# A hybrid decoder layer on one core: dilated attention as near blocks and far token classes, joined by an exchange of maxima and sums

## The chip, the cores and the metric

The kernel runs on one core of a Trainium2 chip. The metric is the device time of one execution in microseconds (us). TensorE multiplies matrices into PSUM, VectorE and ScalarE empty PSUM and do the elementwise work, GpSimd (POOL) works on SBUF, and SyncE (SP) issues the DMAs from one queue.

## The reference

One layer on 1024 tokens with 1024 channels in float32: a pre-norm, one projection into a gated part (256 channels) and the q, k and v of 12 attention heads of 64, an output projection, and a gated convolutional channel mixer. The change touches the attention only:

```python
DILATED_CONFIGS = ((128, 1), (512, 4), (2048, 16))
...
for window, dil in DILATED_CONFIGS:
    o, lse = dilated_segment(q, k, v, rel_bias, window, dil)   # causal; query t attends t, t-d, ..., t-window
    ...
w = jax.nn.softmax(jnp.stack(lses, axis=0), axis=0)
return jnp.sum(w[..., None] * o, axis=0)
```

Combining the three segments by their softmax denominators is one softmax over all keys, in which a key at distance d counts as often as segments contain it: (d <= 128) + (d divisible by 4 and d <= 512) + (d divisible by 16). The count's logarithm is added to the logit with the relative-position bias. So a query sees every token of the last 128 and, farther back, only tokens whose distance is divisible by 4. With 1024 tokens, d divisible by 16 is never cut off.

## The kernel before, in words

Numbers are split into a high and a low part of TensorE's fp32r type, so that products are made of two or three matmuls. After the norm and the transposes of x (hT), the kernel makes the gated part and v (`proj_a`, eight token blocks of 24 matmuls for each half of the v heads, `v_out`), in which three matmul pairs (`bias_mm`) make a table of bias by distance; it is stored in DRAM (`gd`), and `bias_copies` spreads each head's row over 128 rows (`gcop`), from which `load_bias` reads a skewed 128 x 1024 tile.

Then attention runs head by head. `proj_qk` is a list of 48 matmuls of 512 columns (two halves of the tokens, hf 0 and 1, 24 each) which make q and k of one head; after the 24th and the 48th, `evac` empties them and two DMAs copy Kh and Kl to the other 64 partitions. These matmuls are the fill: `pump(n)` puts the next n of them into TensorE's order, at places given by the tables FILL and FILL_AT, so that TensorE has work while other engines finish something. `qk_row` makes the scores of a block of 128 queries with all earlier keys (128 to 1024 columns, in pieces of up to 512), VectorE adds the bias and takes the maximum (L523), ScalarE exponentiates and sums (L528), VectorE takes the reciprocal (L530), POOL rescales the row (L531). `tpv` transposes the weights in batches of up to four blocks (`trans`, L551), splits them (pth, ptl, L555 and L556) and multiplies with v (`pv`, L573) for 256 queries at a time. Scores run one group of two blocks ahead of the values. In heads 10 and 11 `load_wo` brings the output weights through two staging buffers (`raw`), and the first tile of the output projection (`wout_mm`, L630) is the fill of head 11.

The order on TensorE and on SP is the program's own order (`manual_schedule(engines={ET.PE, ET.SP})`); for the other engines a planner orders the instructions ahead of time, and each engine then runs its list strictly in turn.

Of the kernel before, what the change touches and what calls it, by code (L numbers as in the profile page):

```python
# [24 lines left out]
F = mybir.dt.float32  # L26
# [17 lines left out]

FILL = ((0, 11), (4, 6, 3), (3, 7, 2, 4), (0, 3, 2, 1, 2))
FILL_AT = {0: ((9, 4), (4, 2, 5), (6, 2, 5, 0), (0, 1, 4, 1, 5)),
# [3 lines left out]
FILL_FIRST = 4  # L50

# [4 lines left out]
WO_AT = {0: (0, 1), 1: (), 2: (2, 3), 3: (4, 5), 4: (6, 7)}  # L56

L = 1152
NCOP = 128
# [3 lines left out]
def build(tc, x, g1, g2, g3, g4, w_in, ln_g, ln_b, sp_w, sp_b, rel, w_out, w_gate, w_up,  # L63
# [28 lines left out]
    with tc.manual_schedule(engines={ET.PE, ET.SP}), \  # L92
# [39 lines left out]
        ones = cp.tile([1, 128], F, name="ones")  # L132
# [7 lines left out]
        gcop = dr.tile([HEADS, NCOP, L], F, name="gcop")  # L140
# [224 lines left out]
        def bias_load():  # L365
            for c in range(3):
                b = mtile("bb%d" % c)
                sp.dma_start(b[0:32, 0:384], onehot[:, c * 384:(c + 1) * 384])
                sp.dma_start(b[0:12, 384:768], lnm[:, c * 384:(c + 1) * 384])
                sp.dma_start(b[0:32, 768:780], rel)  # L370
                BB.append(b)

        def bias_mm(c):
            b = BB[c]
            p = bS("bias%d" % c)
            pe.matmul(p[:12, :384], b[0:32, 768:780], b[0:32, 0:384], start=True, stop=True)
            dve.tensor_add(b[0:12, 384:768], p[:12, :384], b[0:12, 384:768])

        def bias_store():
            for c in range(3):  # L380
                sp.dma_start(gd[:, c * 384:(c + 1) * 384], BB[c][0:12, 384:768])

        def bias_copies(h):
            sp.dma_start(gcop[h], bass.AP(tensor=gd.tensor, offset=gd.offset + h * L, ap=[[0, NCOP], [1, L]]))

        def v_out(vg, i, p):
            for j in range(3):
# [6 lines left out]
                dve.tensor_sub(vt[:, 1:3, :], src, vt.bitcast(F)[:, 0:4:3, :])  # L394

# [28 lines left out]
        for i in range(NT):  # L424
# [13 lines left out]
            if i in (0, 2, 5):  # L438
                bias_mm(i // 2)
# [7 lines left out]
        def load_qk(h):  # L447
# [7 lines left out]
            for s in range(2):  # L455
                wh = ap.tile([128, 512], R, tag="wqh", name="wqh%d_%d" % (h, s), bufs=4)
                wl = ap.tile([128, 512], R, tag="wql", name="wql%d_%d" % (h, s), bufs=4)
                split(wh, wl, r[:, s * 512:(s + 1) * 512], ENG[WQK_HI[s]], pool)
                WQ[h].append((wh, wl))

        def load_bias(h):
            b = ap.tile([128, T], F, tag="bias", name="bias%d" % h, bufs=2)
            for a in range(0, 128, NCOP):
                sp.dma_start(b[a:a + NCOP], bass.AP(tensor=gcop.tensor, offset=gcop.offset + h * NCOP * L + 127 - a,
                                                    ap=[[L - 1, NCOP], [1, T]]))
            BIAS[h] = b

        def proj_qk(h):
# [15 lines left out]
            def evac(hf):  # L484
                if hf == 0:
                    QK[h] = tuple(ap2.tile([128, T], R, tag="qk", name="%s%d" % (n, h), bufs=4)
                                  for n in ("Q", "Kh", "Kl"))
                q, kh, kl = QK[h]
                p = st[hf]
                s = slice(hf * 512, (hf + 1) * 512)  # L490
                act.activation(kh[64:128, s], p[64:128], AF.Copy)
                act.activation(q[0:64, s], p[0:64], AF.Copy, scale=0.125)
                dve.tensor_sub(kl[64:128, s], p[64:128], kh.bitcast(F)[64:128, s])
                dve.scalar_tensor_tensor(q[64:128, s], p[0:64], 0.125, q.bitcast(F)[0:64, s],  # L494
                                         op0=OP.mult, op1=OP.subtract)
                sp.dma_start(kh.bitcast(F)[0:64, s], kh.bitcast(F)[64:128, s])
                sp.dma_start(kl.bitcast(F)[0:64, s], kl.bitcast(F)[64:128, s])
# [10 lines left out]
        CH = {4: (256, 384), 5: (384, 384), 6: (384, 512), 7: (512, 512)}  # L508

        def qk_row(h, b):  # L510
            q, kh, kl = QK[h]
            w = 128 * (b + 1)
            t = ap2.tile([128, T], F, tag="row", name="row%d_%d" % (h, b), bufs=4)
            c0 = 0
            nm = 3.0e38
            for n in CH.get(b, (w,)):
                p = bS("s%d_%d_%d" % (h, b, c0))
                qs = q[:, b * 128:(b + 1) * 128]
                pe.matmul(p[:, :n], qs, kh[:, c0:c0 + n], start=True, stop=False)  # L519
                pe.matmul(p[:, :n], qs, kl[:, c0:c0 + n], start=False, stop=True)  # L520
                nn = stat("nm%d_%d_%d" % (h, b, c0))
                o = 128 * (7 - b) + c0
                dve.tensor_tensor_reduce(t[:, c0:c0 + n], p[:, :n], BIAS[h][:, o:o + n], -1.0, nm,  # L523
                                         op0=OP.add, op1=OP.min, accum_out=nn)
                nm = nn
                c0 += n
            z = stat("z%d_%d" % (h, b))
            act.activation(t[:, :w], t[:, :w], AF.Exp, bias=nm, scale=-1.0, accum_out=z)  # L528
            rz = stat("rz%d_%d" % (h, b))
            dve.reciprocal(rz, z)  # L530
            pool.tensor_scalar(t[:, :w], t[:, :w], rz, 1.0, op0=OP.mult, op1=OP.mult)  # L531
            ROW[h, b] = t

        def qk_group(h, g):
            qk_row(h, 2 * g)
            qk_row(h, 2 * g + 1)

        def tpv(h, g, nfill):
            pair, odd = divmod(h, 2)
            if h % 2 == 0 and g == 0:  # L540
                mixT[2 + pair] = mtile("mix%d" % (2 + pair))
            r0, r1 = ROW.pop((h, 2 * g)), ROW.pop((h, 2 * g + 1))
            PT = {}

            def trans(u):
                p = bP("pt%d_%d_%d" % (h, g, u))
                j = 2 * u
                n = 4 if u < g else 3
                srcs = [(r0, j), (r1, j)] + ([(r0, j + 1), (r1, j + 1)] if u < g else [(r1, j + 1)])
                for a, (r, jj) in enumerate(srcs):  # L550
                    pe.transpose(p[:, a * 128:(a + 1) * 128], r[:, jj * 128:(jj + 1) * 128], ident)  # L551
                hi = ap.tile([128, 512], R, tag="pth", name="pth%d_%d_%d" % (h, g, u), bufs=3)
                lo = ap.tile([128, 512], R, tag="ptl", name="ptl%d_%d_%d" % (h, g, u), bufs=2)
                n *= 128
                act.activation(hi[:, :n], p[:, :n], AF.Copy)  # L555
                dve.tensor_sub(lo[:, :n], p[:, :n], hi.bitcast(F)[:, :n])  # L556
                PT[u] = (hi, lo)

            pump(nfill[0])
            trans(0)  # L560
            pump(nfill[1])
# [695 lines left out]
```

## Time and profile before

| | us |
|---|---|
| median of 3 runs (lowest, highest) | 1196.83 (1196.66, 1197.32) |
| the profiled execution | 1199.82 |
| its span, first to last instruction | 1198.1 |
| TensorE busy | 1163.6 (97%) |
| VectorE, ScalarE, POOL busy | 839.7, 582.9, 370.6 |
| from the first projection of a head (148 us) to the last values (464 us) | 316 |
| mean TensorE clock granted | 0.992 of full |

PE is TensorE's matmuls and PEld its weight loads, which overlap with them; DVE is VectorE, ACT ScalarE. A matmul's length in the trace includes its way through the array, so that successive ones overlap: the distance between their starts says what one costs. In the table of stages, the numbers after the stage's length are each engine's busy time and, in brackets, its instructions.

### The profile page before, as it was taken

What the parts mean: (1) busy time and instruction counts of PE and PEld (TensorE: products, weight loads), DVE (VectorE), ACT (ScalarE), POOL (GpSimd) and SP (SyncE); (2) the same over time, 40 slices, a digit from 0 to 9 for tenths busy, and PEclk for the clock granted to TensorE, in tenths of its full rate; (3) what the DMA queues carried; (4) which work ended last, traced back from release to release, by engine and by line L of the source; (5) the groups of instructions that cost most, each with busy time, mean ns of one, the idle gap of its engine ahead of it and who ended that gap; (6) DMA issues with size and microseconds to landing.
All of it is one profiled execution on the core that took longest, in us unless ns stands there. A gap on an engine that the chain in (4) does not pass through costs nothing.

```text
span 1198.1 us, 16554 instructions
## 1 busy us (share of the span) xinstructions
PE 1163.6 (97%) x5691; PEld 976.8 (82%) x5691; DVE 839.7 (70%) x1559; ACT 582.9 (49%) x1174; POOL 370.6 (31%) x402
## 2 busy tenths in 40 slices
PE   7899999999999999999999999999999999999996
PEld 5789978888887878887788888888888888888884
DVE  5752257777777775468997678777777679779665
ACT  5532256667765664457534243432434345446521
POOL 2850023334323374234033313332133310000451
PEclk9999999999999999999999999999999999999998
DMA  5323133343233442251143323433143289334345
GB/s 180 106 59 89 25 83 73 91 117 84 73 78 76 108 141 71 92 173 53 36 132 97 115 67 117 132 97 106 62 132 106 88 302 357 97 97 129 110 130 203
DMA packets 107420, 134.31 MB, mean 112 GB/s; under 512 B 30779, under 2 KB 74311, under 8 KB 107336
## 3 DMA queue, kind: packets, MB, share of 16 engines
q1 hardware_dynamic: 105032, 131.15, 35.9%
q10 hardware_dynamic: 2304, 2.10, 0.5%
q8 instruction: 45, 0.74, 0.3%
q14 instruction: 39, 0.32, 0.1%
HBM read 98.30 MB, written 35.71 MB: 112 GB/s over the span
## 4 chain that ended last, share of the span: by engine, by line
PE 86%; DVE 5%; DMA 3%; POOL 2%; ACT 2%; issue 2%; SPq 0%; DVEq 0%; POOLq 0%; ACTq 0%
PE d L996 15%; PE qk L479 10%; PE y L630 7%; PE o L573 4%; PE pt L551 4%; PE s L519 2%; PE s L520 2%; PE v L242 2%; PE v L244 2%; PE v L243 2%; PE Bu L857 2%; PE Au L856 2%; PE Au L857 2%; PE Au L855 2%; PE Bu L856 2%; PE Bu L855 2%
## 5 line engine op out<-in xcount | busy, mean ns | idle before, releaser
L996 PE MATMUL d<-t,s 128*128 128x512 f32 x924 | 211.9, 391 | 1.9 <-ACT t L73 1.6
L996 PEld LDWEIGHTS d<-t,s 128*128 128x128 f32 x924 | 174.5, 189 | 39.2 <-ACT t L73 2.0
L531 POOL TENSOR_SCALAR row<-row,rz 128x128 f32<-128x128 f32 (+3 forms) x96 | 72.8, 759 | 213.2 <-DVE rz L530 200.2
L528 ACT ACTIVATE row<-row,nm 128x128 f32<-128x128 f32 (+3 forms) x96 | 74.4, 775 | 49.0 <-DVE nm L523 48.7
L556 DVE TENSOR_TENSOR ptl<-pt,pth 128x512 fp32r<-128x512 f32 (+1 forms) x120 | 75.7, 634 | 19.6 <-ACT pth L555 18.3
L630 PE MATMUL y<-woh,ms 128*128 128x512 f32 x256 | 82.8, 396 | 0.4 <-DVE Q L494 0.4
L555 ACT ACTIVATE pth<-pt 128x512 fp32r<-128x512 f32 (+1 forms) x120 | 65.8, 550 | 33.3 <-PE pt L551 31.9
L479 PE MATMUL qk<-hTh,wqh 128*128 128x512 f32 x192 | 81.1, 422 | 0.0
L73 ACT ACTIVATE s<-sf 128x512 fp32r<-128x512 f32 x77 | 48.2, 626 | 65.7 <-PE d L996 26.4
L479 PE MATMUL qk<-hTl,wqh 128*128 128x512 f32 x192 | 78.7, 410 | 0.0
L479 PE MATMUL qk<-hTh,wql 128*128 128x512 f32 x192 | 76.6, 399 | 0.0
L78 DVE TENSOR_TENSOR s<-sf,s 128x512 fp32r<-128x512 f32 x77 | 53.5, 695 | 24.0 <-ACT s L73 23.9
L551 PE MATMUL pt<-ident,row 128*128 128x128 f32 x432 | 68.4, 274 | 1.6 <-POOL row L531 1.5
L1011 POOL TENSOR_TENSOR x<-x,g4t 128x512 f32<-128x512 f32 x12 | 18.4, 1536 | 158.0 <-DMA g4t<-in_norm_ffn_post 133.8
L73 ACT ACTIVATE wtg<-tg 128x512 fp32r<-128x512 f32 x44 | 27.5, 632 | 80.9 <-PE Cu L857 67.8
L805 POOL TENSOR_TENSOR tu<-wu 128x512 f32<-128x512 f32 x11 | 17.5, 1590 | 156.1 <-PE Ag L857 74.5
L908 DVE SCALAR_TENSOR_TENSOR c<-G,cols,c 128x1023 f32<-128x1023 f32 (+1 forms) x44 | 57.7, 1329 | 6.7 <-ACT c L906 6.7
L523 DVE CUSTOM_DVE_ANT_0 row<-s,bias 128x384 f32<-128x384 f32 (+2 forms) x96 | 49.9, 519 | 17.7 <-PE s L520 11.8
L551 PEld LDWEIGHTS pt<-ident,row 128*128 128x128 f32 x432 | 51.3, 140 | 10.4 <-POOL row L531 2.5
L73 ACT ACTIVATE wtu<-tu 128x512 fp32r<-128x512 f32 x44 | 27.6, 630 | 64.2 <-PE Cg L857 50.8
L630 PEld LDWEIGHTS y<-woh,ms 128*128 128x128 f32 x256 | 47.9, 188 | 10.8 <-issue 0.8
L573 PE MATMUL o<-ptl,V 128*128 128x256 f32 x240 | 49.4, 287 | 4.8 <-DVE ptl L556 4.5
(329 smaller groups left out, 3232.5 us busy)
## 6 DMA issues: line engine op xcount, KB each, us to landing
sf<-sD SPq DMA_DIRECT2D x77, 256.0 KB, 2.8
wu<-in_w_up SPq DMA_DIRECT2D x11, 1024.0 KB, 5.0
wd<-in_w_down SPq DMA_DIRECT2D x22, 512.0 KB, 7.0
wg<-in_w_gate SPq DMA_DIRECT2D x10, 1024.0 KB, 6.0
sD<-c SPq DMA_DIRECT2D x30, 256.0 KB, 6.5
gcop<-gd SPq DMA_DIRECT2D x12, 576.0 KB, 4.8
wqk<-in_w_in SPq DMA_DIRECT2D x24, 256.0 KB, 6.0
bias<-gcop SPq DMA_DIRECT2D x12, 512.0 KB, 4.1
```

The source lines that it names most:

```text
L73: act.activation(hi, src, AF.Copy)
L78: lo_eng.tensor_sub(lo, src, hi.bitcast(F))
L479: pe.matmul(st[hf], w, m, start=k == 0 and j == 0, stop=k == KT - 1 and j == 2)
L528: act.activation(t[:, :w], t[:, :w], AF.Exp, bias=nm, scale=-1.0, accum_out=z)
L531: pool.tensor_scalar(t[:, :w], t[:, :w], rz, 1.0, op0=OP.mult, op1=OP.mult)
L551: pe.transpose(p[:, a * 128:(a + 1) * 128], r[:, jj * 128:(jj + 1) * 128], ident)
L555: act.activation(hi[:, :n], p[:, :n], AF.Copy)
L556: dve.tensor_sub(lo[:, :n], p[:, :n], hi.bitcast(F)[:, :n])
L573: pe.matmul(ov, v, t[:, s], start=j == 0 and x == 0, stop=x == 1 and j == 2 * g + 1, skip_group_check=True)
L630: pe.matmul(YP[i, hf], m, w, start=k == 0 and j == 0, stop=k == KT - 1 and j == 2)
L908: dve.scalar_tensor_tensor(c[:, d:T], g[:, 0:T - d], col(2 - d, f), c[:, d:T], op0=OP.mult, op1=OP.add)
L996: pe.matmul(b, l, r, start=first and n in FIRST and q == 0, stop=last and n in LAST and q == 2, skip_group_check=True)
```

## The change

Scores are computed only where the softmax can have weight. For each head there are two sets of blocks:

- near: query blocks of 128 successive tokens against their own and the previous 128 keys, for distances up to 128: 15 blocks of 128 x 128 instead of 36;
- far: tokens sorted into four classes by their number modulo 4, 256 tokens each; each class has two query blocks, against the class's keys up to there: 12 blocks. The near distances are masked out there by the bias.

Each set has a maximum and a sum of its own for every query. The two sets hold a query at different places (in near, partition r x 32 + c of a block; in far, 128 tokens of one class), so `stat_out` transposes the 128 x 32 table of maxima and sums, stores it to DRAM in three DMAs and loads it back with the other set's order in three; `stat_in` transposes it back, forms the common weight with eight small VectorE operations and two exponentials, and POOL rescales all 16 pieces of rows. Reciprocals of every block are gone. Scores of head h+1 are made within head h (`attend(h, h + 1)`).

Further: q, k are stored by class, with a near copy Qn of q (four VectorE copies per half); v is stored to DRAM in both orders (`vN`, `vC`) by five DMAs for each half of a head pair, and `load_v` brings each pair back with four loads; the bias table has 2440 columns instead of 1152 and is made by five matmul pairs instead of three; bias copies are 32 rows of 2048 and 128 rows of 392 columns instead of 128 of 1152; the projections run two heads ahead of the values instead of one, so head 10 has no fill; all of `load_wo` stands at the start of head 10; head 11 has two tiles of the output projection as fill instead of one.

The core of the diff:

```diff
-FILL = ((0, 11), (4, 6, 3), (3, 7, 2, 4), (0, 3, 2, 1, 2))
...
+FILL = (2, 2, 2, 3, 3, 3, 5, 7, 8, 8, 99)
+FILL_LAST = (6, 6, 6, 7, 7, 8, 8, 8, 9, 9, 99)
...
         def load_qk(h):
...
-                wh = ap.tile([128, 512], R, tag="wqh", name="wqh%d_%d" % (h, s), bufs=4)
+                wh = ap.tile([128, 512], R, tag="wqh", name="wqh%d_%d" % (h, s), bufs=3)
...
             def evac(hf):
...
+                q, kh, kl = [cls(t)[:, :, hf * 128:(hf + 1) * 128] for t in QK[h][:3]]
+                p = st[hf].rearrange("p (a r) -> p r a", r=4)
...
+                qn = QK[h][3][:, hf * 512:(hf + 1) * 512].rearrange("p (b r c) -> p b r c", b=4, r=4)
+                qf = q.bitcast(F).rearrange("p r (b c) -> p b r c", b=4)
+                for b in range(4):
+                    dve.tensor_copy(qn[:, b], qf[:, b])
...
+        def logits(h, x, u):
...
+            for y in range(4 if u and x == 0 else 2):
+                if u == 0:
+                    b = 2 * x + y
+                    a0, n = (0, 1) if b == 0 else (32 * (b - 1), 2)
+                    qs = qn[:, 128 * b:128 * (b + 1)]
+                    ks = [cls(k)[:, :, a0:a0 + 32 * n].rearrange("p r (x c) -> p r x c", x=n) for k in (kh, kl)]
+                    c = slice(256 * y, 256 * y + 128 * n)
...
+                else:
+                    r, h2 = (y, 0) if x == 0 else (2 * (x - 1) + y, 1)
+                    n = 128 * (h2 + 1)
+                    qs = q[:, 256 * r + 128 * h2:256 * r + 128 * (h2 + 1)]
+                    ks = [k[:, 256 * r:256 * r + n] for k in (kh, kl)]
...
+                for w in range(2):
+                    pe.matmul(sh(p[:, c]), qs, ks[w], start=w == 0, stop=w == 1, skip_group_check=True)
+                parts.append((c, bs, i))
+            for c, bs, i in parts:
+                nm, z = SA[h][:, i:i + 1], SA[h][:, i + 8:i + 9]
+                dve.tensor_tensor_reduce(t[:, c], p[:, c], bs, -1.0, 3.0e38, op0=OP.add, op1=OP.min,
+                                         accum_out=nm)
+                act.activation(t[:, c], t[:, c], AF.Exp, bias=nm, scale=-1.0, accum_out=z)
...
+        LG = [(0, 0), (1, 0), (0, 1), (2, 0), (3, 0), (1, 1), (2, 1)]
...
+        def stat_out(h):
+            p = bP("sx%d" % h)
+            pe.transpose(p[0:32, 0:128], SA[h], ident)
+            x1 = ap2.tile([32, 128], F, tag="sx", name="sx%d" % h, bufs=1)
+            dve.tensor_copy(x1, p[0:32, 0:128])
...
+            for s_ in range(2):
+                sp.dma_start(at(1024 * s_, (32, 8), (256, 4), (1, 32)),
+                             x1[8 * s_:8 * s_ + 8].rearrange("b (r q) -> b r q", r=4))
+            sp.dma_start(at(2048, (128, 16), (1, 128)), x1[16:32])
+            y = ap2.tile([32, 128], F, tag="sy", name="sy%d" % h, bufs=1)
+            SY[h] = y
+            sp.dma_start(y[16:32], at(0, (128, 16), (1, 128)))
+            for s_ in range(2):
+                sp.dma_start(y[8 * s_:8 * s_ + 8].rearrange("b (r q) -> b r q", r=4),
+                             at(2048 + 1024 * s_, (32, 8), (256, 4), (1, 32)))
+
+        def stat_in(h):
+            p = bP("sy%d" % h)
+            pe.transpose(p[:, 0:32], SY[h], ident[0:32, 0:32])
...
+            dve.tensor_tensor(v(m), oth[:, :, 0], own[:, :, 0], op=OP.min)
...
+            act.activation(e[:, 0:16], d[:, 0:16], AF.Exp)
+            act.activation(e[:, 16:32], d[:, 16:32], AF.Exp, scale=-1.0)
...
+            dve.tensor_mul(w, e[:, 0:16], z1)
+            for x, u in LG:
+                t = ROW[h, u, x]
+                for y in range(4 if u and x == 0 else 2):
...
+                    pool.tensor_scalar(t[:, c], t[:, c], w[:, i:i + 1], 1.0, op0=OP.mult, op1=OP.mult)
...
+        BATCH = [[(0, 0), (1, 0), (1, 1), (2, 1)], [(2, 2), (3, 2), (3, 3), (4, 3)], [(r, 0, 0) for r in range(4)],
+                 [(4, 4), (5, 4), (5, 5), (6, 5)], [(6, 6), (7, 6), (7, 7)],
+                 [(r, 1, k) for r in (0, 1) for k in (0, 1)], [(r, 1, k) for r in (2, 3) for k in (0, 1)]]
...
+        def attend(h, ahead):
...
+            trans(h, 0); lg(0); fp(); lg(1); fp(); trans(h, 1); lg(2); fp(); pv(h, 0); lg(3); fp()
+            trans(h, 2); lg(4); fp(); pv(h, 1); lg(5); fp(); trans(h, 3); lg(6); pv(h, 2); fp()
+            trans(h, 4); pv(h, 3); fp()
+            stat_out(ahead)
+            trans(h, 5); pv(h, 4); fp(); trans(h, 6); pv(h, 5); fp()
+            stat_in(ahead)
+            pv(h, 6); fp()
...
+        load_v(0)
         fill.extend(proj_qk(0))
         pump(48)
...
+        for x_ in range(7):
+            logits(0, *LG[x_])
+            pump(4)
+        stat_out(0)
+        pump(18)
+        stat_in(0)
         for h in range(HEADS):
...
+            pump(len(fill))
+            if h + 2 < HEADS:
+                fill.extend(proj_qk(h + 2))
+            elif h + 2 == HEADS:
+                for k in range(KT):
+                    load_wo(k)
...
+            attend(h, h + 1)
```

Here `attend` is written several calls to a line. `fp()` pumps the next number of FILL (of FILL_LAST in head 11, which has no head ahead and so no `lg`, `stat_out` and `stat_in`). The batches are numbered from 0: values 0 to 4 are mostly near, 5 and 6 far.

More of the change, by code (lines that the diff above doesn't have):

```diff
@@ L506, in pump @@
                     fill.popleft()()
[L508 to L532, printed above, removed]
@@ L539, in tpv, with pv @@
+        def pv(h, s):
             pair, odd = divmod(h, 2)
-            if h % 2 == 0 and g == 0:
+            if h % 2 == 0 and s == 0:
                 mixT[2 + pair] = mtile("mix%d" % (2 + pair))
[L542 to L557, printed above, removed]
@@ new lines, in pv @@
+            for x in range(2):
+                t = PT[h, s][x]
+                for v, a, n, h2, at in jobs:
+                    first = (h, h2) not in OB
+                    if first:
+                        OB[h, h2] = (bO if h2 == 0 else bS)("o%d_%d" % (h, h2))
+                    o = at(OB[h, h2])
+                    src = t[:, 128 * a:128 * (a + n)]
+                    if len(o.shape) == 4:
+                        src = src.rearrange("p (x r c) -> p x r c", r=4, c=32)
+                        if n == 1:
+                            o, src = o[:, 0], src[:, 0]
+                    pe.matmul(o, v[:, odd * 128:(odd + 1) * 128], src, start=first, stop=x == 1 and s in (2, 6),
+                              skip_group_check=True)
@@ L632, in wout_mm, with fp, lg @@
             return [mm(hf, k, j) for k in ks for hf in range(2) for j in range(3)]
+        def attend(h, ahead):
+            fl = iter(FILL if ahead < HEADS else FILL_LAST)
+            def fp():
+                pump(next(fl))
+            def lg(x):
+                if ahead < HEADS:
+                    logits(ahead, *LG[x])
+            trans(h, 0)
+            lg(0)
+            fp()
+            lg(1)
+            fp()
+            trans(h, 1)
+            lg(2)
+            fp()
+            pv(h, 0)
+            lg(3)
+            fp()
+            trans(h, 2)
+            lg(4)
+            fp()
+            pv(h, 1)
+            lg(5)
+            fp()
+            trans(h, 3)
+            lg(6)
+            pv(h, 2)
+            fp()
+            trans(h, 4)
+            pv(h, 3)
+            fp()
+            if ahead < HEADS:
+                stat_out(ahead)
+            trans(h, 5)
+            pv(h, 4)
+            fp()
+            trans(h, 6)
+            pv(h, 5)
+            fp()
+            if ahead < HEADS:
+                stat_in(ahead)
+            pv(h, 6)
+            fp()
@@ L1104, in build @@
                 hs_sums(0, 2)
-            for f in wout_mm(i, range(KT), bS if c % 2 else bD):
+            for f in wout_mm(i, range(KT) if c > 1 else [KT - 1], bS if c % 2 else bD):
                 f()
```

258 lines of the change are left out of this document (157 added, 101 removed), and 3 rows, old and new, of the table FILL_AT.

## The prediction

> **What bounds the kernel now.** I read the page's engine table, the chain, then a table of stages, and last the order of instructions on TensorE and on SP's queue inside one head.
>
> ```profile
> span 1198.1 us, 16554 instructions
> PE 1163.6 (97%) x5691; PEld 976.8 (82%) x5691; DVE 839.7 (70%) x1559; ACT 582.9 (49%) x1174; POOL 370.6 (31%) x402
> ...
> PE 86%; DVE 5%; DMA 3%; POOL 2%; ACT 2%; issue 2%; SPq 0%; DVEq 0%; POOLq 0%; ACTq 0%
> ```
>
> ```profile
> core 0: us, PE busy (x) PEld busy (x) DVE busy (x) ACT busy (x) POOL busy (x), PEclk, DMA share, GB/s
> 148.00:464.00 316.00, 308.40 (x1820) 264.61 (x1820) 226.07 (x622) 206.43 (x441) 117.87 (x134) 0.99 0.35 88
> 253.02:277.73 24.71, 24.71 (x150) 21.29 (x149) 18.10 (x51) 17.07 (x37) 8.67 (x11) 1.00 0.37 89
> 414.00:418.00 4.00, 3.80 (x22) 3.13 (x22) 2.80 (x10) 1.96 (x6) 1.28 (x2) 1.00 0.95 341
> 369.00:371.00 2.00, 0.93 (x5) 0.93 (x6) 1.09 (x3) 0.00 (x0) 1.01 (x2) 0.89 0.31 66
> 371.00:373.00 2.00, 2.00 (x6) 1.57 (x5) 1.70 (x5) 0.00 (x0) 0.16 (x1) 0.50 0.00 0
> 373.00:375.00 2.00, 2.00 (x11) 1.68 (x10) 1.01 (x2) 1.20 (x3) 0.00 (x0) 0.76 0.00 0
> ```
>
> The change lives between 148 and 464 us. There TensorE idles 7.6 of 316 us, and one head (24.71 us) has no idle at all, with VectorE at 18.1 and ScalarE at 17.1. So attention is bound by TensorE's instruction stream; any wait put into that stream is paid in full.
>
> What one matmul costs is the distance between starts, not its length:
>
> ```profile
> 253.02 0.22 PE L519 MATMUL s<-Kh,Q 128*128 128x128 f32 x1
> 253.08 0.27 PE L520 MATMUL s<-Kl,Q 128*128 128x128 f32 x1
> 253.19 0.33 PE L519 MATMUL s<-Kh,Q 128*128 128x256 f32 x1
> 253.36 0.28 PE L520 MATMUL s<-Kl,Q 128*128 128x256 f32 x1
> 253.48 0.34 PE L573 MATMUL o<-pth,V 128*128 128x256 f32 x2
> ...
> 249.91 0.60 PE L551 MATMUL pt<-ident,row 128*128 128x128 f32 x4
> 250.26 0.48 PE L479 MATMUL qk<-hTl,wqh 128*128 128x512 f32 x1
> 250.58 0.39 PE L479 MATMUL qk<-hTh,wql 128*128 128x512 f32 x1
> 250.81 0.40 PE L573 MATMUL o<-pth,V 128*128 128x256 f32 x2
> ```
>
> ```profile
> 253.02 0.19 PEld L520 LDWEIGHTS s<-Kl,Q 128*128 128x128 f32 x1
> 253.13 0.19 PEld L519 LDWEIGHTS s<-Kh,Q 128*128 128x128 f32 x1
> 253.24 0.19 PEld L520 LDWEIGHTS s<-Kl,Q 128*128 128x128 f32 x1
> ```
>
> 512 columns take 0.23 us (250.58 to 250.81), 256 take 0.12 (253.36 to 253.48), 384 by estimate between them 0.17. 128 columns start 0.06 after one another, but weight loads are never closer than 0.11, and the loss shows one matmul later (253.19 to 253.36 is 0.17 for 256 columns). Four transposes take 0.35 and make the next matmul 0.09 dearer: 0.11 each. So I price 128 columns at 0.11, nearly as much as 256. That decides what the change saves.
>
> **TensorE work, per head.** Before, projection is 48 x 0.23 = 11.0. Scores are 24 matmuls (2 x (0.11 + 2 x 0.12 + 5 x 0.17 + 4 x 0.23)) = 4.2; values are 32 x 0.12 + 8 x 0.11 = 4.7; 36 transposes are 4.0. The sum is 23.9, against 24.7 measured. After, scores are 22 matmuls of 256 and 10 of 128 columns, 3.7; values are 12 of 256 and 30 of 128, 4.7; 27 transposes and two for the exchange are 3.2. A quarter of the score blocks goes, but matmuls get narrower: the saving is 1.3 us a head, 15 over 12 heads. Its other end: at 0.06 for 128 columns it would be 2.8 a head, 33.
>
> **The exchange, first wait.** The statistics of head h+1 go out at stat_out and must be back at stat_in, inside head h. On the way are a transpose, a VectorE copy, three stores, three loads that depend on them, and everything ahead on SP's queue.
>
> ```profile
> 282.88 0.39 PE L479 MATMUL qk<-hTh,wql 128*128 128x512 f32 x1
> ...
> 285.58 0.46 SPq L497 DMA_DIRECT2D Kl<-Kl  x1
> ```
>
> ```profile
> 105.44 0.29 SPq L381 DMA_DIRECT2D gd<-bb  x1
> 108.43 0.57 SPq L384 DMA_DIRECT2D gcop<-gd  x1
> ...
> Kh<-Kh SPq DMA_DIRECT2D x24, 128.0 KB, 2.2
> ...
> wo<-in_w_out SPq DMA_DIRECT2D x8, 512.0 KB, 3.6
> ```
>
> The 24th fill is the fourth of the seven just ahead of stat_out, and its K copies are queued on SP before the stores. SP issues the Kl copy 2.70 after the last projection matmul starts (282.88 to 285.58) and needs 0.46, so it is free 0.69 + 2.70 + 0.46 - 1.61 = 2.2 us after the transpose. Three issues of 0.3 put the third store at +0.6. A dependent read of DRAM starts 2.99 after the store it reads (105.44 to 108.43). Three loads: the last +0.6 later, landing 2.2 after. With 0.1 to TensorE: 2.2 + 0.6 + 3.0 + 0.6 + 2.2 + 0.1 = 8.7. Cover on TensorE between the two transposes: two batches of transposes 0.88, values 4 and 5 1.34, 16 fills 3.68, own 0.1: 6.0. Wait: 2.7 a head. Ends: 0 if SP is free and the stores overlap; 4.2 if the VectorE copy stands behind the evacuation of Q and the four new copies. I take 2.7, the sum of rows. Ten heads (0 to 9): +27. Behind sy's transpose on TensorE stand the last values and fills, which could have run; behind SP's wait for the stores only the next K copies, due 13 fills later.
>
> **The exchange, second wait.** After stat_in come eight small VectorE operations, two exponentials, and 16 rescales on POOL; formerly each row was rescaled as soon as it was ready, heads ahead of need.
>
> ```profile
> 24.30 0.17 DVE L298 TENSOR_SCALAR mm<-mu 128x4 f32<-128x4 f32 x1
> ...
> L528 ACT ACTIVATE row<-row,nm 128x256 f32<-128x256 f32 x12 | 6.0, 501 | 0.8 <-DVE nm L523 0.8
> L531 POOL TENSOR_SCALAR row<-row,rz 128x256 f32<-128x256 f32 x12 | 5.7, 478 | 13.5 <-DVE rz L530 13.5
> L78 POOL TENSOR_TENSOR wol<-wo,woh 128x512 fp32r<-128x512 f32 x14 | 18.4, 1330 | 4.2 <-DVE woh L77 4.2
> ```
>
> Transpose 0.3, eight operations at 0.17 and a gap 1.6, two exponentials 0.5 (estimate, below the 256-column row), three rescales before the first batch of transposes is whole 1.4, four changes of engine at 0.1: 4.2 us. Cover: the last values 0.9, five fills 1.2, and the transposes that trickle 0.5: 2.6. Wait 1.6. The second batch needs the ninth rescale, 2.5 us after the third, with 2.0 of TensorE work between: another 0.4. Together 2.0 a head; ends 1.2 (VectorE operations half as long) and 3.0 (half as long again). Ten heads: +20.
>
> **Start of attention.** V now goes to DRAM twice and comes back: 60 stores (12.6 MB). Those of the second half are issued on SP ahead of the first K copies, and the last six MB can only leave after about 143 us; at the 341 GB/s of the table 8 MB (with load_v) take 24 us. Between 0 (hidden) and 13 us late for the first scores; I take 5, since SP's issues alone cost 3. The bias table is five matmul pairs of 488 columns, not three of 384; a 0.74 us pair stands in the chain:
>
> ```profile
> 87.61 0.74 PE bias L376 x2
> ```
>
> That is 0.74 x (5 x 488 / 384 - 3) = +2.5. Head 0's exchange has 18 fills of cover and then 2: waits 2.9 + 3.6 = 6.5.
>
> **Heads 10 and 11.** Head 10 has no fills: the projections ran one head earlier. All eight load_wo stand before it on SP, with two staging buffers (3.6 landing, an estimated 0.6 of split, 2 x 1.33 on POOL). The last is issued 20 to 24 us into the head, and the statistics queue behind it: 22 + 6.5 + 4.2 = 32.7 us for 11.6 us of work, 21 idle. Head 11 has 84 output matmuls as fill; those of the second tile are only moved, sum zero. What goes in return: all idle of the stage before, 7.6, and 1.7 of slowed clock behind a stall (0.11, 0.50 and 0.24 of 2 us each).
>
> Cost nothing: smaller bias loads, load_v's four on every second head, and their SP issues (asked for two heads ahead; else 2 us a head), the third wqh buffer (its split is due a dozen fills later), strided evacuation of Q and K and four VectorE copies (VectorE's 18.1 grows to an estimated 21 us of a 28 us head; else 2 us).
>
> **Sum.** -15 + 27 + 20 + 5 + 2.5 + 6.5 + 21 - 9.3 = +57.7. The profiled execution ran 1199.8 us, 0.25% over the median; as a difference, the sum goes onto the median of 1196.8: 1254 us.
>
> **Rivals.** *The exchange is hidden* (chance 0.19, the side of faster). The small transfers overlap better than the gd row, the chain behind stat_in fits under the last fills, and neither holds up heads 0 to 10. Then -15 + 5 + 2.5 + 4 (head 10 alone, on ScalarE) - 9.3 = -13: 1184. It decides once both waits together are under about 1 us a head and head 10 isn't held. For it: the queue carries little at that point (88 GB/s over the stage). Against it: SP's order is fixed, and 2.99 and 2.2 are rows of an unloaded queue.
>
> *The clock drops too* (0.20).
>
> ```profile
> 370.07 0.50 PE L573 MATMUL o<-ptl,V 128*128 128x256 f32 x2 [2.68 <-DVE ptl L556]
> ```
>
> That one gap of 2.68 us was followed by a granted clock of 0.89, 0.50, 0.76 (371 to 373 lowest), 1.7 us lost. Gaps of 2.7 and 1.6 in each head may do the same; part of the slow time lies under the second wait, so about 1 us a head, +10: 1264. The Trainium skill, TensorE: Matmul & The Clock Gate, Part 1, lets the clock halve after at least one idle window of about 3.4 us; by that rule gaps of 2.7 leave it alone and 1254 stands. The trace differs: the row above has it halved after 2.68.
>
> *Runs of 32 columns in PSUM are dear* (0.08). Near scores and values, 34 matmuls a head, write PSUM in pieces of 32. No row shows such a write; if each took a 512 slot, 34 x 0.11 x 12 = +45: 1299. The Trainium skill, SBUF — State Buffer, section Door 1: The DMA port swizzle, says that non-contiguous PSUM patterns slow matmuls down a lot; no run here shows it yet.
>
> **How the numbers follow.** My forecast has 0.50; 0.03 is left for no change. Faster by over 0.2% (what this kernel's runs can tell apart) 0.19, within it 0.03, slower 0.78. The range takes half of the first rival and all of the clock: 1190 to 1292; the forecast's own is 1225 to 1285 (first wait 1.5 to 4, start 0 to 13).
>
> **What would show it.** TensorE idle ahead of the transposes of sy (by a DMA) near 2.7 us a head, ahead of pt by POOL near 2; s and o of 128 columns at 0.11 apart; a head of 27 to 28 us; head 10 over 30 with SP waiting for wol; first K copy landing after 160. The prediction is wrong if sy finds its data there, if a head falls below 24, or if 128 columns run at 0.06.

## The result and the profile after

The changed kernel takes 1275.63 us (median of 4 runs, 1273.18 to 1278.43) against 1197.07 (4 runs, 1196.66 to 1200.0) for the kernel before, run beside it: 1.0651 times as long, 95% interval 1.0623 to 1.068. It is 78.6 us slower.

The head of the page of the kernel after, as shown above for before:

```profile
span 1271.5 us, 17193 instructions
PE 1167.7 (92%) x5731; PEld 973.2 (77%) x5731; DVE 835.1 (66%) x1705; ACT 576.8 (45%) x1330; POOL 381.9 (30%) x498
PE 68%; DMA 5%; DVE 4%; POOL 3%; issue 3%; ACT 2%; SPq 2%; DVEq 0%; POOLq 0%; ACTq 0%
```

The span grew by 73.4 us and TensorE's busy time by 4.1: nearly everything added is TensorE standing still, and its share of the chain fell from 86% to 68%. (The 4.1 are 13.4 more of slowed clock less 9.3 of work, as the next paragraph shows.) The list of TensorE's waits says for what (line, what was waited for, total us, times, longest):

```profile
PE sy L598 <- DMA sy<-sX: 21.9, 12, 12.5
PE pt L660 <- POOL row L633: 20.4, 12, 4.3
PE s L562 <- DMA Kh<-Kh: 17.6, 1, 17.6
PE hT L887 <- DVE xb L875: 7.5, 1, 7.5
```

From 140 us to the first transposes of the output part (476.56 before, 548.85 after, 72.3 apart) I added up slices of half a us, each with its busy time and its granted clock. TensorE idles 76.0 us against 7.6 before; 15.1 us of its busy time are lost to a slowed clock against 1.7; what is left, its work at full clock, is 317.9 against 327.2. That is 68.4 + 13.4 - 9.3 = 72.5. The 9.3 hold both ends of a trade: up to the first projection of a head (148.00 before, 152.61 after) the work is 2.5 larger, by the longer bias table, and from there on 11.8 smaller. After the transposes the two kernels differ by 1 us.

**The start.** The timeline of the kernel after, SP's queue and then TensorE:

```profile
147.14 0.54 SPq L404 DMA_DIRECT2D vC<-V  x1
147.72 3.16 SPq L407 DMA_DIRECT2D vN<-V  x4
...
167.19 2.84 SPq L407 DMA_DIRECT2D vN<-V  x4
...
172.39 0.64 SPq L516 DMA_DIRECT2D Kh<-Kh  x1
...
181.26 0.45 PE L562 MATMUL s<-Kh,Qn 128*128 128x128 f32 x1 [17.57 <-DMA Kh<-Kh]
```

In the kernel before, the first scores stood here, without a wait:

```profile
158.94 0.22 PE L519 MATMUL s<-Kh,Q 128*128 128x128 f32 x1
```

SP needs about 0.7 us for each store of vN. Six groups of five stores (147.14 to 170.03), then load_v, stand ahead of the first K copy, which TensorE awaits for 17.57 us. Two things are in this wait. The copy is issued late, at 172.39. And it is slow: it ends the wait 8.9 us after its issue, where the K copies of the kernel before land in 2.2. In the trace the last of load_v's four loads, 2 MB issued just ahead of it, is complete at 180.36 and the copy at 181.13.

**One exchange, in the middle of attention** (timeline of TensorE, SP, VectorE and POOL, in order of time):

```profile
328.33 0.27 PE L576 MATMUL sx<-ident,sa 128*32 128x128 f32 x1
329.85 0.62 SPq L517 DMA_DIRECT2D Kl<-Kl  x1
330.52 0.85 SPq L586 DMA_DIRECT2D sX<-sx  x2
331.42 0.32 SPq L588 DMA_DIRECT2D sX<-sx  x1
332.74 0.31 SPq L591 DMA_DIRECT2D sy<-sX  x1
333.16 0.63 SPq L593 DMA_DIRECT2D sy<-sX  x2
335.19 0.21 PE L598 MATMUL sy<-ident,sy 32*128 32x32 f32 x1 [0.65 <-DMA sy<-sX]
337.17 1.06 DVE L704 TENSOR_TENSOR mix<-o,ot 64x512 f32<-64x512 f32 x1 [0.28 <-ACT ot L703]
338.07 0.16 DVE L622 TENSOR_TENSOR w<-e,z 128x16 f32<-128x16 f32 x1
338.35 6.87 POOL L633 TENSOR_SCALAR row<-row,w 128x128 f32<-128x128 f32 x16 [3.96 <-DVE w L622]
338.77 1.23 PE L660 MATMUL pt<-ident,row 128*128 128x128 f32 x4 [1.14 <-POOL row L633]
```

From the one transpose to the other it takes 6.9 us, from there to the first batch of transposes 3.6. Over the ten exchanges of heads 0 to 9 the first wait is 8.8 us in all (0.46 to 1.27 each), the second 12.0 (1.10 to 1.38).

**Head 10, and slowed clock.** Windows of the kernel after (columns as before; the last three are granted clock, DMA share, GB/s):

```profile
309.21:335.19 25.98, 23.87 (x152) 20.18 (x152) 17.52 (x62) 16.22 (x49) 9.44 (x18) 1.00 0.34 71
467.17:502.70 35.53, 18.11 (x108) 15.55 (x109) 20.72 (x69) 18.62 (x57) 26.31 (x34) 0.77 0.40 128
257.00:264.00 7.00, 5.90 (x22) 4.27 (x21) 5.27 (x17) 3.04 (x8) 5.34 (x13) 0.53 0.35 58
```

Between two exchanges a middle head takes 26 us with 23.9 of work; head 10 takes 35.5 with 18.1 busy. Its rows in the timeline of TensorE and SP, and behind them a wait at the end of attention that is new:

```profile
480.37 16.57 SPq L725 DMA_DIRECT2D wo<-in_w_out  x6
502.70 0.28 PE L598 MATMUL sy<-ident,sy 32*128 32x32 f32 x1 [12.51 <-DMA sy<-sX]
509.18 1.14 PE L660 MATMUL pt<-ident,row 128*128 128x128 f32 x3 [4.30 <-POOL row L633]
...
548.85 1.94 PE L887 MATMUL hT<-ident,xb 128*128 128x128 f32 x8 [7.46 <-DVE xb L875]
```

SP is held for 16.57 us by the loads of the output weights (they wait for staging buffers), and the statistics stand behind them. The wait at 548.85 is at a place where before had none:

```profile
476.56 1.03 PE L728 MATMUL hT<-ident,xb 128*128 128x128 f32 x8
```

### The profile page after: what moved, and what is told of

The parts are those of the page before. It is cut to its first block, busy times and chain, and to the rows that moved or that the text cites. A ratio compares the mean times of both kernels' runs of the same rounds, so it can differ in the third digit from the quotient of the medians.

```text
span 1271.5 us, 17193 instructions
## 1 busy us (share of the span) xinstructions
PE 1167.7 (92%) x5731; PEld 973.2 (77%) x5731; DVE 835.1 (66%) x1705; ACT 576.8 (45%) x1330; POOL 381.9 (30%) x498
## 4 chain that ended last, share of the span: by engine, by line
PE 68%; DMA 5%; DVE 4%; POOL 3%; issue 3%; ACT 2%; SPq 2%; DVEq 0%; POOLq 0%; ACTq 0%
PE d L1155 14%; PE y L748 7%; PE qk L499 6%; PE s L562 3%; PE o L696 3%; PE pt L660 2%; PE Bu L1016 2%; PE Au L1016 2%; PE Au L1015 2%; PE Au L1014 2%; PE Bu L1015 2%; PE Bu L1014 2%; PE Cu L1015 1%; PE Ag L1015 1%; PE Cg L1015 1%
## 5 line engine op out<-in xcount | busy, mean ns | idle before, releaser
L568 ACT ACTIVATE row<-row,sa 128x128 f32<-128x128 f32 (+1 forms) x192 | 89.2, 467 | 36.4 <-DVE sa L566 35.6
L633 POOL TENSOR_SCALAR row<-row,w 128x128 f32<-128x128 f32 (+1 forms) x192 | 82.7, 457 | 66.7 <-DVE w L622 66.7
L77 POOL TENSOR_TENSOR wql<-wqk,wqh 128x512 fp32r<-128x512 f32 x24 | 30.9, 1288 | 218.0 <-ACT wqh L72 124.4
L566 DVE CUSTOM_DVE_ANT_0 row<-s,bias 128x128 f32<-128x128 f32 (+1 forms) x192 | 64.5, 378 | 46.0 <-PE s L562 29.2
L665 DVE TENSOR_TENSOR ptl<-pt,pth 128x512 fp32r<-128x512 f32 (+1 forms) x84 | 56.2, 669 | 37.4 <-ACT pth L664 36.8
L660 PE MATMUL pt<-ident,row 128*128 128x128 f32 x324 | 58.7, 293 | 22.1 <-POOL row L633 20.4
L499 PE MATMUL qk<-hTh,wqh 128*128 128x512 f32 x192 | 78.2, 407 | 0.0
L660 PEld LDWEIGHTS pt<-ident,row 128*128 128x128 f32 x324 | 41.9, 146 | 43.0 <-POOL row L633 32.7
L77 DVE TENSOR_TENSOR s<-sf,s 128x512 fp32r<-128x512 f32 x77 | 53.0, 689 | 23.4 <-ACT s L72 23.2
L664 ACT ACTIVATE pth<-pt 128x512 fp32r<-128x512 f32 (+1 forms) x84 | 48.2, 574 | 43.1 <-PE pt L660 42.0
L964 POOL TENSOR_TENSOR tu<-wu 128x512 f32<-128x512 f32 x11 | 17.4, 1585 | 155.9 <-PE Ag L1016 104.2
L748 PEld LDWEIGHTS y<-woh,ms 128*128 128x128 f32 x256 | 49.5, 195 | 10.2
```

The source lines that it names most:

```text
L77: lo_eng.tensor_sub(lo, src, hi.bitcast(F))
L499: pe.matmul(st[hf], w, m, start=k == 0 and j == 0, stop=k == KT - 1 and j == 2)
L566: dve.tensor_tensor_reduce(t[:, c], p[:, c], bs, -1.0, 3.0e38, op0=OP.add, op1=OP.min, accum_out=nm)
L568: act.activation(t[:, c], t[:, c], AF.Exp, bias=nm, scale=-1.0, accum_out=z)
L633: pool.tensor_scalar(t[:, c], t[:, c], w[:, i:i + 1], 1.0, op0=OP.mult, op1=OP.mult)
L660: pe.transpose(p[:, a * 128:(a + 1) * 128], src, ident)
```

## The experiments

Each is the kernel after with one edit, unless said otherwise. In each the kernel before was timed on the same chip (1197.8 to 1198.8); the ratios are to it. For the kernel after the ratio is 1.0651.

**Half of the V stores later.** The stores of the second half go into heads 0 to 5, and load_v(0) goes behind the first K copies, so this run changes both.

```diff
-                    v = V.pop((pr_, i // 4)) ...; sp.dma_start(vC ...); 4 x sp.dma_start(vN ...)
+                    if vg == 0:
+                        v_store(pr_, i // 4)      # the same five stores
...
         for h in range(HEADS):
+            if h < 6:
+                v_store(3 + h // 2, h % 2)
...
-        load_v(0)
         fill.extend(proj_qk(0))
         pump(48)
+        load_v(0)
```

> The stores of v for the second half of the heads are issued one group a head within heads 0 to 5, and load_v(0) behind the first K copies; all arithmetic stays. Theory (SP's order is what holds the first scores: the K copies stand behind 30 stores and 4 loads): the wait of s for Kh, 17.6 us, falls below 3 us and the kernel gets 14 to 17 us faster, about 1260. Rival (the DMA engines are full at that time and the K copies are slow wherever they stand, or the stores give it back inside the heads through SP): the wait falls by a few us or the heads grow, gain below 6 us.

Measured 1261.31 (1258.7 to 1263.92), ratio 1.0532 [1.0477, 1.0588]: 14 us less. The wait of 17.57 us is gone from the list, and the first scores come at 161.91; part of the wait came back in heads 1, 3 and 5, where load_v stands too (timeline, SP and TensorE):

```profile
339.88 0.87 SPq L589 DMA_DIRECT2D sX<-sx  x2
...
346.24 0.31 SPq L594 DMA_DIRECT2D sy<-sX  x1
...
348.50 0.28 PE L601 MATMUL sy<-ident,sy 32*128 32x32 f32 x1 [4.61 <-DMA sy<-sX]
```

Here the read back is issued 6.4 us after the first store, not 2.2 as at 330.52 above: by the order of SP's rows, the stores stand behind the transfers of V issued just before them.

**No second copy of V.**

```diff
-                    for t in range(4):
-                        sp.dma_start(vN[pr_, r0:r0 + 128].rearrange("(r q) c -> q r c", r=4), v[:, t])
...
+                        for r in range(4):      # load_v, near order, from vC
+                            sp.dma_start(t.bitcast(F)[32 * r:32 * r + 32],
+                                         half_.rearrange("(t q r) c -> r q t c", t=4, r=4)[r])
```

> The second copy of V in DRAM is not stored (48 stores of 128 KB fewer); the near-part tiles are read from the first copy, in four loads for every half instead of one. Theory: the late first scores (17.6 us) come from SP, which needs about 0.7 us to issue each of those stores and has the first K copies behind 24 of them. With 24 x 0.7 = 17 us less and 6 loads x 0.5 = 3 us more ahead of the K copies, the wait falls to about 4 us, and the time to about 1262. Rival: the bytes bound the start, not the issues; 3 of 14 MB go, the wait falls by a fifth, to 14 us, and the time to 1272.

Measured 1278.05 (1277.57 to 1278.54), ratio 1.0661 [1.0615, 1.0707]: nothing gained, though the wait at the start fell from 17.57 to 6.33 (the theory had 4), and one at sy grew (timeline of SP and TensorE):

```profile
163.21 0.69 SPq L513 DMA_DIRECT2D Kh<-Kh  x1
...
170.63 0.45 PE L559 MATMUL s<-Kh,Qn 128*128 128x128 f32 x1 [6.33 <-DMA Kh<-Kh]
...
248.79 0.28 PE L595 MATMUL sy<-ident,sy 32*128 32x32 f32 x1 [3.93 <-DMA sy<-sX]
```

So SP's issues of the stores held most of the start: the K copy is issued 9.2 us earlier, and the wait is 11.2 us shorter. Their bytes did not; by them the rival had 14 us left, and in the kernel after the last store is complete 2.2 us after its issue (169.42 to 171.61). The 6.33 that stay go with the slow copy: it still takes 7.4 us from its issue, behind the same 2 MB of load_v. The gain went into the exchanges of every second head: ten loads instead of four now stand ahead of them, with waits of 3.93, 3.63, 1.81 and 4.77 us at sy in heads 1, 3, 5 and 7, and slowed clock behind them. The wait moved; neither time that was forecast came.

**Staging of the output weights.** Eight buffers of their own instead of two shared ones:

```diff
         def load_wo(k):
-            r = raw("wo%d" % k)
+            r = mtile("wor%d" % k)
```

> The output weights are staged in eight tiles of the large pool instead of the two raw buffers, so that their loads no longer wait for POOL's splits. Theory (head 10's statistics stand behind load_wo on SP): the 12.5 us wait of sy in head 10 falls to 3 to 6 us and the kernel gains 7 to 10 us, about 1267. Rival (POOL's 19 us of splits hold head 10, since the rescales stand behind them): the wait moves from sy to pt and the gain is below 3 us.

Measured 1274.29 (1273.27 to 1275.32), ratio 1.0641 [1.061, 1.0672]. SP is free, sy finds its data (at 495.94), and the time hardly changes (timeline of VectorE, POOL and TensorE):

```profile
495.68 6.37 DVE L76 CAST woh<-wor 128x512 fp32r<-128x512 f32 x6
...
507.89 0.16 DVE L609 TENSOR_TENSOR m<-sy,sa 128x16 f32<-128x16 f32 x1
...
511.74 6.74 POOL L633 TENSOR_SCALAR row<-row,w 128x128 f32<-128x128 f32 x16 [3.44 <-DVE w L622]
512.17 1.14 PE L660 MATMUL pt<-ident,row 128*128 128x128 f32 x3 [14.02 <-POOL row L633]
```

The number is that of the rival, its path is not. POOL has its splits of the weights ahead of the rescales, but it is through with them and idle for 3.44 us when w comes. VectorE's list has splits of the output weights and of the mixed values ahead of the exchange's first operation: m comes 12 us after sy's transpose. So the wait passed from SP's queue to VectorE's list. Six casts in it take 6.37 us, which take 2.08 in the next experiment (at 486.49); why they are slow here is not shown. In the kernel after it is the same in small: w of head 10 is done at 508.66, with POOL idle for 3.51 us before.

**Fewer splits in head 10.** The same buffers; only three of the eight weights are split in head 10, the others issued behind it:

```diff
                 for k in range(KT):
                     load_wo(k)
+                for k in range(3):
+                    split_wo(k)
             else:
+                for k in range(3, KT):
+                    split_wo(k)
```

> The loads of the output weights go to eight buffers of their own, so that SP does not wait; only three of their splits are issued in head 10, the other five after it. Theory: head 10 waits for two things in turn, SP behind the loads (12.5 us at sy) and POOL behind the splits (14 us at pt once SP is free). With both gone head 10 takes 20 to 24 us instead of 35.5, and the time is about 1262. Rival: POOL's 2.6 us of split for each weight block are only moved; the output matmuls of head 11 then wait for them, and the time stays at 1270 or more.

Measured 1266.69 (1264.61 to 1268.78), ratio 1.0566 [1.0491, 1.0641]: 9 us less, of some 13 expected, from two runs, and the interval still touches that of the kernel after. The planner that orders POOL and VectorE drew the later splits forward (timeline, VectorE, then POOL):

```profile
495.54 0.16 DVE L609 TENSOR_TENSOR m<-sy,sa 128x16 f32<-128x16 f32 x1
495.62 4.05 DVE L76 CAST ms<-mix 128x128 fp32r<-128x128 f32 x4
...
503.15 0.18 DVE L622 TENSOR_TENSOR w<-e,z 128x16 f32<-128x16 f32 x1
486.40 12.78 POOL L77 TENSOR_TENSOR wol<-wor,woh 128x512 fp32r<-128x512 f32 x8 [0.40 <-DVE ptl L665]
```

From m to w it takes 7.6 us, where a middle head takes 2.9 from sy's transpose to w, since the splits of the mixed values stand between; and m itself comes 4.8 us after sy's transpose (490.72). pt waits 11.0 us for it.

**Cover for the end.** Half of the second output tile's matmuls are kept until the first tile's end is under way (FILL_LAST is lowered to match):

```diff
-                    fill.extend(wout_mm(i, range(KT - 1), bS if i else bD))
+                    fill.extend(wout_mm(i, range(3) if i else range(KT - 1), bS if i else bD))
...
-  range(KT) if c > 1 else [KT - 1]
+  range(KT) if c > 1 else range(3, KT)
```

> Of the second tile of the output projection only three of seven row groups are fill in head 11; the other 24 matmuls go back behind the first tile's end. Theory (the 7.5 us wait of hT at the end of attention, and the halved clock after it, are work that was taken away as cover): the wait falls to about 2 us, head 11 is shorter by the 24 matmuls, gain 7 to 10 us, about 1267. Rival (the wait comes from the planner's order on VectorE and POOL): gain below 2 us.

Measured 1266.79 (1265.83 to 1267.75), ratio 1.0578 [1.0547, 1.0609]: 8.8 us less; the wait at hT falls from 7.46 to 2.06. The theory held.

**No trip through DRAM.**

```diff
-            for s_ in range(2): sp.dma_start(at(...), x1[8 * s_:8 * s_ + 8]...)   # and four more transfers
+            SY[h] = x1
```

> The six DMAs of the exchange are left out: stat_in transposes the kernel's own table back, so each set is normalised with itself and half of every weight is wrong; all else, the second wait too, stays. Theory (the first wait is the DRAM trip): no wait at sy but for the VectorE copy, heads shorter by 0.6 to 1.2 us, 10 us over heads 0 to 9, and head 10's 12.5 us gone: 1253 to 1256. Rival (the trip only shows the wait that a backlog on VectorE and ScalarE would make anyway): heads as long as before, only head 10 gains, about 1263.

Measured 1265.14 (1264.67 to 1265.6), ratio 1.0564 [1.0534, 1.0595]: 10.5 us less. No wait at sy is left. From head to head it is 25.3 us (9 heads, 228.75 to 456.79) against 26.5 (228.96 to 467.17). So in a middle head the trip costs 1.1 us, 0.3 of it in slowed clock, and the second wait stands. What head 10 saves, head 11 partly loses: its output matmuls then wait 3.84 us for VectorE and 3.63 us for POOL.

**No exchange at all.**

```diff
                 act.activation(t[:, c], t[:, c], AF.Exp, bias=nm, scale=-1.0, accum_out=z)
+                dve.reciprocal(rz, z)
+                pool.tensor_scalar(t[:, c], t[:, c], rz, 1.0, op0=OP.mult, op1=OP.mult)
...
-                stat_out(ahead)
-                stat_in(ahead)
```

> Each near and each far piece is divided by its own sum at once (a reciprocal on VectorE, a rescale on POOL); the joining of the two parts (the exchange with its two transposes, six transfers and eight small operations) is left out, so the output is not attention over the joint softmax. Theory: the split of the scores itself pays, and only the joining costs. Then the TensorE waits for the rescales (20.4 us over 12) and for the exchange (21.9 over 12) go, a head takes the 23.4 to 24 us of its own work, below the 24.5 of the kernel before, and the time is 1275.6 - 42 - 6 (head 0) = about 1228 us, of which 17.6 are the late first scores and 9 the uncovered end, still there. Rival: narrower matmuls and strided operands cost what the removed blocks save; a head stays at 24.5 or more and the time at 1240 or more.

Measured 1240.12 (1239.0 to 1241.24), ratio 1.0345 [1.03, 1.0389]. The first scores of heads 2 and 11 in this kernel, then of heads 3 and 8 in the kernel before (timelines):

```profile
228.42 0.30 PE L562 MATMUL s<-Kh,Qn 128*128 128x128 f32 x1
436.90 0.30 PE L562 MATMUL s<-Kh,Qn 128*128 128x128 f32 x1
```

```profile
228.66 0.22 PE L519 MATMUL s<-Kh,Q 128*128 128x128 f32 x1
351.02 0.22 PE L519 MATMUL s<-Kh,Q 128*128 128x128 f32 x1
```

A head takes 208.48 / 9 = 23.2 us against 122.36 / 5 = 24.5 before: the split itself pays 1.3 us a head, and the theory holds for the heads. The exchange costs 26.5 - 23.2 = 3.3 us a head, 1.1 for the trip and 2.2 for what follows. Over the whole kernel, leaving it out is worth 35.5 of the 78.6 us. The total is 12 us over the forecast of 1228: TensorE comes early to the output projection and waits 17.9 us for the splits of the mixed values. The work around head 10 is a limit of its own.

**Later fills.**

```diff
-FILL = (2, 2, 2, 3, 3, 3, 5, 7, 8, 8, 99)
+FILL = (1, 1, 1, 1, 1, 2, 4, 5, 11, 11, 99)
```

> Only the counts of projection matmuls between the steps of a head change: 16 instead of 27 before the statistics go out, 22 instead of 16 between their going out and coming back, 10 instead of 5 after it. Theory: the two waits of a head (0.5 to 1.3 us and 1.1 to 1.4 us) are a lack of cover on TensorE; 6 more matmuls of 0.23 us in the first gap and 5 more in the second take both to near zero in heads 0 to 9, and with nothing new the time falls by 10 to 20 us, to about 1260. Rival: the cover is only taken from the first part of the head, where the scores then wait for their PSUM buffers and for VectorE; or the evacuation of Q and K, now issued after the statistics, comes ahead of the small operations on VectorE. Then the time stays at 1270 or more, and new waits by VectorE stand at the scores or at sy.

Measured 1269.04 (1267.08 to 1271.01), ratio 1.0586 [1.0515, 1.0657]: 6.6 us less, from two runs, and the interval still touches that of the kernel after. One head of it (timeline):

```profile
335.18 1.24 PE L660 MATMUL pt<-ident,row 128*128 128x128 f32 x4 [0.48 <-POOL row L633]
...
349.76 0.63 PE L660 MATMUL pt<-ident,row 128*128 128x128 f32 x4 [0.60 <-DVE sx L578]
```

sy finds its data (at 331.09) and pt waits 0.5 instead of 1.1; a new wait of 0.60 by VectorE's copy of sx appears. A head is 26.0 us. Both theories were partly right: cover was lacking, but the waits at sy and pt fall only from 42.3 to 35.3 us in all, 5.0 of the new kind among them.

**Rescales on two engines.**

```diff
-                    pool.tensor_scalar(t[:, c], t[:, c], w[:, i:i + 1], 1.0, ...)
+                    if (x + y) % 2: act.activation(t[:, c], t[:, c], AF.Copy, scale=w[:, i:i + 1])
+                    else: pool.tensor_scalar(...)
```

> Of the 16 rescales of a head, those with odd x + y go to ScalarE, the others stay on POOL; nothing else changes. Theory: the wait at pt (1.1 to 1.4 us in heads 0 to 9) is the time of three rescales in a row on POOL behind w; with every second one on ScalarE it falls by about 0.5 us a head and by more in head 0 (4.04), so the time falls by 5 to 8 us, to about 1269. Rival: the eight small operations and two exponentials ahead of w carry the wait, and ScalarE's own queue (evacuations of pt, exponentials) delays the rescales given to it; then the time stays within 2 us of 1275.6.

Measured 1276.8 (1273.96 to 1279.63), ratio 1.0658 [1.0624, 1.0692]: nothing. The rival held: pt waits for the first rescale, and that for w; 1.10 to 1.31 us in heads 0 to 8, as before.

**All repairs together.** The stores and class-order loads of V behind the exchange, later fills (in head 0 too), rescales on two engines, mixed values split ahead of head 10, three weights loaded in head 10 and five in head 11, cover for the end.

> The change with every repair together: half of the V stores moved behind heads 0 to 5, load_v(0) behind the first K copies, in later pairs the class-order half of V loaded behind the exchange; 16, 22 and 10 projection matmuls before, inside and after the exchange; every second rescale on ScalarE; splits of the mixed values ahead of head 10, three output weights loaded in head 10 and five in head 11; half of the second output tile kept as cover for the first one's end. Theory: the gains of the single repairs add (14 start, 9 end, 7 cover, 5 rescales, 10 to 15 head 10): 1275.6 - 48 = about 1228, still slower than before, since each head keeps one to two us around the exchange. Rival: they share one another's time (what is late next takes it), and less than half arrives: 1250 or more. For a version that beats the kernel before it would have to be under 1195.

Measured 1267.91 (1265.44 to 1271.45), ratio 1.0587 [1.056, 1.0615]. The rival held: of 48 us, 8 arrived. The timeline of ScalarE and TensorE shows what ate them:

```profile
304.14 3.09 ACT L637 ACTIVATE row<-row,w 128x256 f32<-128x256 f32 x8 [1.34 <-DVE w L625]
...
311.31 0.51 PE L704 MATMUL o<-ptl,Vn 128*128 128x256 f32 x2 [1.80 <-DVE ptl L673]
```

Eight rescales in a row hold ScalarE for 3.09 us; pth and ptl come late (waits of 0.60 and 1.80 us in each head), and with the fills moved away nothing covers it. The same rescales alone cost nothing, where the early fills stood.

**All repairs, rescales on POOL.** As above, with `pool.tensor_scalar` for every rescale again.

> The kernel of all repairs, with the 16 rescales of a head back on POOL; all else as in that kernel. Theory: in it eight rescales in a row took ScalarE 3.09 us a head, ahead of the evacuation of K and Q and of the transposed batches, and TensorE waited 0.6 us for pth and 1.8 us for ptl in each head, with half clock behind it. With them on POOL these waits go, the heads come to about 26 us as with the later fills alone (29 to 30 in the kernel of all repairs), and the time is about 1275.6 - 14 (start) - 9 (end) - 7 (cover) - 12 (head 10) = 1234; still above 1197. Rival: the o waits come from too little work between the transposes and the values (one projection matmul where there were two), not from ScalarE's rescales; then they stay, and the time stays near 1268.

Measured 1234.04 (1228.08 to 1236.21), ratio 1.0306 [1.0276, 1.0335]: 41.6 us less than the kernel after, as forecast, and no head from 0 to 9 waits at o for pth or ptl any more. Exchanges of heads 0 and 9 in the timeline:

```profile
208.15 0.24 PE L601 MATMUL sy<-ident,sy 32*128 32x32 f32 x1
442.26 0.24 PE L601 MATMUL sy<-ident,sy 32*128 32x32 f32 x1
```

A head is 26.0 us (234.11 / 9). This is the fastest version with the whole computation; it does not reach the kernel before.

**All repairs and no exchange.** The repairs of start, head 10 and end, with the fills where they were, and each piece divided by its own sum; a bound for a cheaper exchange in this order of work:

> The same repairs of start, head 10 and end, and each piece divided by its own sum at once: the joining of the two parts is left out, so the output is not attention over the joint softmax. It is the bound for any cheaper exchange. Theory: 1240 - 14 (start) - 9 (end) - 8 to 12 (head 10) = about 1207: even with a free exchange the change would not beat the 1197 of before, as 16.6 us of smaller head work go against the larger start, the wait for the output weights, and what else is left. Rival: heads of 23.1 us (against 24.5) are worth all of 16 us, the rest is repaired in full, and the time is 1185 to 1195, faster than before.

Measured 1200.55 (1199.51 to 1202.73), ratio 1.002 [1.0009, 1.0031]. TensorE is busy for 1150.7 us, 96% of the span: nearly as full as before, with 13 us less to do, and the time is 0.2% above it: the first scores come at 164.50 instead of 158.94, the next head's K copies are awaited for 4.8 us, and the output matmuls for their weights; these take what the smaller heads give.

## Why the prediction was right in sign and in kind, and where its sum was wrong

The forecast of 1254 us was 21.6 below the 1275.63 measured: slower, because waits come into TensorE's stream, by 57 against 78.6. But the exchange, which carried most of the forecast (27 + 20 + 6.5), is only a third of what was measured (8.8 + 12.0 + 6.3). Step by step:

| step | forecast | measured |
|---|---|---|
| TensorE work in the heads | -15 (1.3 a head) | -11.8 at full clock; 1.3 a head without the exchange |
| bias pairs | +2.5 | +2.5 |
| first wait, ten heads | +27 | +8.8 |
| second wait, ten heads | +20 | +12.0 |
| start of attention | +5 | +17.6 |
| wait for V at 148.37, ahead of the first projection | none | +2.1 |
| head 0's exchange | +6.5 | +4.7 (0.66 and 4.04), and 1.55 ahead of its first transpose, which the step did not have |
| head 10, idle | +21 | +20.3 (17.4 up to sy, of which 1.4 belong to the row above, and 4.3 at pt) |
| end, "only moved, sum zero" | 0 | +7.5 |
| clock slowed behind gaps | given back, -1.7 | +13.4 |

With the 7.6 us of old idle given back, the measured terms come to 71.1 of the 72.3 us up to the transposes; 1.1 more lie behind them (the medians lie 78.6 apart).

**Held.** 128 columns do cost 0.11: the starts of the far scores, and 256 columns in the near ones (timeline of after):

```profile
316.63 0.27 PE L562 MATMUL s<-Kh,Q 128*128 128x128 f32 x1
316.74 0.28 PE L562 MATMUL s<-Kl,Q 128*128 128x128 f32 x1
...
318.29 0.28 PE L562 MATMUL s<-Kh,Qn 128*128 128x256 f32 x1
318.40 0.28 PE L562 MATMUL s<-Kl,Qn 128*128 128x256 f32 x1
```

The near ones write PSUM in runs of 32 columns and take 0.11 to 0.12, as the plain ones did: the third rival is refuted. What the Trainium skill says in SBUF — State Buffer, section Door 1: The DMA port swizzle, of matmuls slowed by non-contiguous PSUM patterns does not show in these runs. Head 10's time went as described, with SP held by the loads of the weights and then 4.30 us at pt; but w came late there by VectorE's splits, which the step did not have.

**First wait: mis-sized.** The mechanism is right, and so is its first step (SP free 2.1 us after the transpose; forecast 2.2). The dependent read was taken from the gd row at 2.99 us after its store; it is 1.32 (331.42 to 332.74). The last load lands within 1.5 us of its issue start, not 2.2. With 6.9 us of trip instead of 8.7 and 6.2 of cover, 0.65 is left of 2.7.

**Second wait: mis-sized.** 3.6 us instead of 4.2, because transposes start behind the first rescale, not the third; and the wait for the ninth does not appear. VectorE's list has a mix operation of 1.06 us ahead of w, which no step had foreseen.

**Start: mis-sized, for a reason that was there.** The step priced the stores by their bytes and put SP's issues at 3 us. They are 24 stores of 0.7 us in the second half alone, in order, ahead of the K copies; without them the copy is issued 9.2 us earlier and the wait is 11 us shorter. The rest is the copy's own way behind load_v's 2 MB, 8.9 us instead of the 2.2 that the step had from its row. The time lay beyond the step's own end of 13.

**End: the failed step.** "Those of the second tile are only moved, sum zero" counted matmuls and not what they covered: before, they stood in front of the transposes that wait for the first tile's end. The run with the cover put back gained 8.8, 5.4 of it at this wait.

**Clock: a rival that was half the truth.** It was priced at gaps of 2.7 and 1.6 us in every head. The gaps are 0.9 and 1.2 us on average, and only three of the ten exchanges show it: the clock falls to half at 257.4, 366.6 and 472.4 us, behind waits of 1.0 to 1.4, and 6.3 of the 15.1 us are lost there. The others lie behind the long gaps at the start (2.0), in head 0's exchange (2.0) and in head 10 (4.8), which no term charged for. The Trainium skill, TensorE: Matmul & The Clock Gate, Part 1, names idle windows of about 3.4 us; here gaps of 1.3 us were followed by half clock, and others of the same length were not.

So two terms were 26 us too large and three (start, end and clock) 35 us too small, and the saving was put 3 us too high: that the total came within its range is luck, as errors of both signs largely cancelled. The rival that the exchange is hidden would have given 1184. The kernel with no exchange at all takes 1240.12, and 1200.55 with start, head 10 and end repaired as well: in this order of work, hiding the exchange alone would not have made the change faster.

## What to carry to other kernels

When work is moved off an engine that bounds, ask of every moved instruction what it had covered where it stood, and price each new transfer by the queue that issues it, in order, and by what is in flight ahead of it, not by its bytes alone. A wait taken away can pass to the next list in line (in head 10 from SP's queue to VectorE's splits), so count such a repair only when the one behind it is repaired too. Run the bound first: the kernel with the exchange left out said at once how much the idea could be worth.

## What the hardware showed beside this

A read of DRAM that depends on small stores was issued 2.2 us after the first of them in a middle head, and 6.4 us after where transfers of V stood just ahead. SP takes 0.3 us to issue one transfer of the statistics and 0.7 for one 128 KB store of vN. Half clock followed TensorE gaps as short as 1.3 us, and in the kernel after its stretches up to 560 us last 3.4, 6.8, 10.2, 17.1 or 20.5 us, all close to multiples of 3.4.
